# Emitting the search of blocks 2 and 3 to its end with the last four tiles of the first projection piece, ahead of the long search

## The chip, the cores and the metric

One core of a Trainium2 chip runs the whole kernel. Its engines are TensorE (PE, with PEld for its weight loads), VectorE (DVE), ScalarE (ACT), GpSimd (POOL) and SyncE (SP, which only issues DMAs here). The metric is the device time of one execution in microseconds; the time of a kernel is the median over its runs.

## What is computed

One decoder layer of 1024 tokens with 1024 channels in float32: a SwiGLU feed-forward block with LayerNorm, a token mixer with LayerNorm, a second SwiGLU block with LayerNorm. The part that matters is the mixer's sparse attention:

```
def block(i):                         # 128 queries; blocks i = 0..7
    t = i * 128 + arange(128)
    causal = key_pos[None, :] <= t[:, None]
    logit = einsum('bqhd,bsd->bqhs', qib, ki) * IDX_DIM ** -0.5
    score = einsum('bqh,bqhs->bqs', wib, relu(logit))      # 4 indexer heads
    score = where(causal[None], score, -inf)
    _, sel = lax.top_k(score, 256)
    ... softmax attention of 8 heads over the 256 selected keys
```

Blocks 0 and 1 have at most 256 causal keys, so nothing has to be chosen there. Blocks 2 to 7 need the 256 largest of 384, 512, 640, 768, 896 and 1024 scores for each query. The other half of the mixer is a gated MLP over chunks of 128 tokens; both halves are multiplied by an output matrix.

## The kernel before

All matmuls are done as three products of a high and a low part (`mm3`: lines 152, 153, 154), with the split made by ACT (high part, line 87) and DVE or POOL (low part, line 88). The program is written as Python that emits instructions in an order; a planner then decides, from the emission order as a rank, from the dependences and from its own times, in which order each engine runs them. An instruction of low rank can so run early where an engine is free and its inputs and buffers are there. SBUF buffers come from shared sets: 21 pages of 4 KB a partition hold nearly all that is named here (scores, relu results, u, v, queries, keys, masks, ranks), and an instruction whose result needs a page waits until one is free. PSUM has four single banks (projections, transposes) and two double ones (index logits, attention scores).

The mixer runs in this order. Tokens are handled in eight tiles of 128.

1. Piece A of the input projection (384 columns: latent, index weights, index key, first 188 columns of v), token tiles 0 to 3 while the first feed-forward block ends (`indexer_operands`, `piece("A")`; 24 matmuls a tile, results taken from PSUM by ACT in lines 1096 to 1100). Index queries and keys of tiles 0 to 3, then `early()`: the scores of blocks 2 and 3, and the short search over them.
2. Tail of the feed-forward block with 1 + 2 + 2 steps of the short search (`PX`), the latent normalisation (`latent`), index queries of tiles 4 to 7.
3. Tiles 4 to 7 of piece A. After each tile: `P0` steps of the short search, the index key of the tile (`keys`, transposes kT, line 719), the scores of the block with that number (`scores`: logits lg in line 703, relu on ACT in line 795, weighting on DVE in lines 798 and 800, causal mask on POOL in line 801).
4. The long search over blocks 7, 5, 4, 6 is added to the list of searches. Pieces B (418 columns: rest of v in line 1133, part of u in line 1134) and C (418 columns: rest of u, line 1141), the gate (sv, line 932) with its normalisation (vn, lines 913 to 918), the attention queries (q, lines 693 to 697), the output product of the gate half (y, xr, line 962), q_abs (qa), and the attention: four pairs of blocks by two groups of heads by two blocks, softmax (sc, line 1000), probabilities transposed (pT) and multiplied with the latent (ol). In between stand `pump(n)` calls, n taken from the lists `B`, `C`, `Q`, `W`, `A`.

A search (`topk`) is a Python generator. Its steps: the first count, 31 rounds, one for each bit of the threshold, a fix, and for each block four steps that make the mask. A round flips a bit (DVE line 845), counts the scores below the trial threshold for each block (on DVE line 826; on ACT line 835 with a sign function for block 3 of the short search and for blocks 7 and 5 of the long one), compares (DVE line 838) and keeps or drops the bit (DVE line 847). The mask's steps are a last sign count (ACT line 876), the mask itself (POOL line 881), the ties (DVE line 885, a scan `rank` in line 887, lines 889 and 891) and the sum (POOL line 892). With block 3 come the two pages that hold the masks of blocks 3 to 7. The short search has 1 + 31 + 1 + 8 = 41 steps, the long one 49.

The call that hands out the steps advances every search that is in the list by one step, so that two searches move in step:

```
def pump(self, n):
    for _ in range(n):
        for g in list(self.bg):
            try:
                next(g)
            except StopIteration:
                self.bg.remove(g)
...
for t, _ in enumerate(piece, 4):      # in indexer_operands: tiles 4 to 7
    self.pump(PAR["P0"])
    keys(t, 1)
    if PAR["SI"]:
        self.scores(t)
```

Of the kernel before, what the change touches and what calls it, by code (L numbers as in the profile page):

```python
# [13 lines left out]
ALU = mybir.AluOpType  # L14
AX = mybir.AxisListType

PAR = {'NP': 21, 'NW': 2, 'NB': 15, 'P0': 3, 'B': [0, 0, 0, 0, 0, 0, 0, 2], 'C': [0, 1, 0, 0, 0, 0, 1, 0], 'Q': [6, 0, 0, 1], 'W': [1, 4, 1, 3, 3, 4, 0, 0], 'A': [3, 0, 4, 3, 2, 3, 0, 5, 2, 0, 3, 1, 0, 1, 0, 2], 'L': 3, 'PN': [1, 1, 1, 1], 'E': 4, 'O': [0, 1, 2, 3], 'AQ': 4, 'D4': 2, 'M7': 2, 'NK': [2, 4, 6, 8], 'AK': 5, 'TP': 0, 'CUT': [384, 0, 512, 256], 'LS': 12, 'LX': 5, 'LP': 5, 'LE': [0, 0, 1, 1, 1, 0, 1], 'SE': 0, 'TE': 1, 'HE': 0, 'W2S': 0, 'W2L': 0, 'HL': 0, 'CV': 1, 'WO': 11, 'S6': 1, 'WJ': 8, 'HJ': 8, 'EO': 1, 'EN': 1, 'PX': [1, 2, 2], 'SI': 1, 'FG': 6, 'XR': [0, 2, 0, 0, 0, 1, 0, 1], 'QA': [0, 0, 0, 1, 0, 0, 0, 1, 0, 1, 0, 0, 0, 0, 0, 0], 'HT': 3, 'KO': [7, 5, 4, 6], 'K1': [1, 1], 'K1B': [4], 'K2': [2], 'K2B': [], 'S1': 1, 'LG': [1, 1, 0, 0, 1, 0, 1, 1, 1, 1, 0, 1, 1, 1], 'XV': [0, 1, 1, 0, 0, 0, 1]}
P = 128
T = 1024
D = 1024  # L20
# [9 lines left out]

N_PAGES = PAR["NP"]
N_W = PAR["NW"]
N_BIG = PAR["NB"]
EARLY = 6
class Net:
# [221 lines left out]
    def ffn(self, name, w13, w2, begin, meanwhile, load_acc, norm, after, side=iter(())):  # L257
# [21 lines left out]
        def left(n):  # L279

            for g, m in plan[len(lefts) : n]:
                if g < EARLY and m in (1, 2):
                    lefts[g, m] = self.parts(first_blocks[g, m], V)
                    continue
                a = blocks[g]
                if m == 6:
                    a[5] = self.page("S", (P, 2, HALF))
                    V.tensor_tensor(a[5], a[7], a[4], ALU.add)
                    a[6] = a[1]
                    V.tensor_tensor(a[7], a[1], a[7], ALU.subtract)  # L290
                    V.tensor_tensor(a[6], a[5], a[1], ALU.subtract)  # L291
                if m == (5 if g else 3):
                    V.tensor_tensor(a[2], a[2], a[6], ALU.subtract)
                    a[3] = a[2]
                lefts[g, m] = self.parts(a[m], E(PAR["LE"][m - 1] if g > 1 else 0))

# [18 lines left out]
        def product(g, m, ps, start=True):  # L315
            now = plan.index((g, m))
            for k in range(4):
# [6 lines left out]
                if k or now > 2 * EARLY + 4:  # L324
                    left(now + (3 if now < 2 * EARLY + 5 else 1 + (k + PAR["LS"]) // 4))
                w, x = lefts[g, m], xs[m, k]
# [44 lines left out]
        def group(g, begun=None):  # L371
# [65 lines left out]
            def out():  # L437
                e = E(PAR["HE"])
                s = c
                e.tensor_tensor(s[:, 0], h2[:, 0], h2[:, 1], ALU.add)  # L440
                e.tensor_tensor(s[:, 1], s[:, 0], h11, ALU.subtract)
                e.tensor_tensor(h2[:, 0], h11, h2[:, 0], ALU.subtract)
                e.tensor_tensor(s4, s[:, 1], h12, ALU.subtract)
                if g < EARLY:
                    nc.sync.dma_start(hid[g, :, 1], h12)
                else:
                    nc.sync.dma_start(hid[g, :, 0:2], h1)
                for i, t in enumerate((h2, s), 1):
                    nc.sync.dma_start(hid[g, :, 2 * i : 2 * i + 2], t)
                nc.sync.dma_start(hid[g, :, 6], s4)  # L450
# [795 lines left out]
```

## Time and profile before

| what | value |
|---|---|
| median of 3 runs | 1772.27 us (1771.32 to 1774.21) |
| profiled execution, its time | 1773.37 us |
| its span, first to last instruction | 1771.7 us |
| mean granted clock of TensorE | 0.995 |
| busy: PE, DVE, ACT, POOL | 1723.8, 1329.5, 791.8, 397.9 us |
| first FFN; mixer; second FFN, about | 0 to 656; 656 to 1120; 1120 to 1772 us |

Times in the profile are microseconds from the span's start. A row of an engine's list in time has the start, the duration, the engine, the line, the operation, the tiles (out<-in) and, in brackets, how long the engine stood idle before it and on whose end. A row of a view of a line or a group has a count behind the x and the durations in ns. A row of the stretches gives the busy time and, in brackets, the number of instructions of each engine.

### The profile page before, as it was taken

The page shows a single profiled execution, that of the slowest core. Times are in us where ns is not written, and L with a number is a line of the kernel's source. Part 1 is how long each engine was busy: PE and PEld are TensorE (multiplying, and loading weights), DVE is VectorE, ACT ScalarE, POOL GpSimd, SP SyncE. Part 2 cuts the span into 40 slices and gives each one's busy share as a digit, 9 for nine tenths or more (in the row PEclk, how much of TensorE's full clock was granted, in tenths as well). Part 3 has the DMA queues.
Part 4 walks back from the last instruction along what each step waited for, and adds up shares of the span by engine and source line. Part 5 has one row for each costly group of instructions (what it writes and reads, how often), then busy time and mean ns, then how long its engine had stood idle before and what let it go on. Part 6 is the DMA issues. An engine that isn't in the chain of part 4 may idle for free.

```text
span 1771.7 us, 22241 instructions
## 1 busy us (share of the span) xinstructions
PE 1723.8 (97%) x8016; PEld 1444.5 (82%) x8016; DVE 1329.5 (75%) x2220; ACT 791.8 (45%) x1347; POOL 397.9 (22%) x288
## 2 busy tenths in 40 slices
PE   8989999999999999999999999999999999999997
PEld 6868778888888888998877888888788888888886
DVE  5779886665895865899879877877777455589586
ACT  5423333423545515777777662452322222355551
POOL 0004332222000361001256321100423222200036
PEclk9999999999999999999999999999999999999999
DMA  7458767757545343224512007335443322753532
GB/s 286 152 223 295 298 257 266 268 197 285 192 126 182 102 160 123 90 87 158 199 54 96 1 1 254 120 119 202 155 166 133 123 90 89 289 194 126 176 101 83
DMA packets 89709, 288.64 MB, mean 163 GB/s; under 512 B 9088, under 2 KB 9600, under 8 KB 85504
## 3 DMA queue, kind: packets, MB, share of 16 engines
q1 hardware_dynamic: 82208, 252.33, 40.3%
q10 hardware_dynamic: 5472, 32.02, 4.5%
q0 software_dynamic: 1920, 2.89, 0.8%
q8 instruction: 63, 1.03, 0.2%
q14 instruction: 46, 0.38, 0.1%
HBM read 195.15 MB, written 89.16 MB: 160 GB/s over the span
## 4 chain that ended last, share of the span: by engine, by line
PE 69%; DVE 8%; ACT 3%; POOL 3%; issue 2%; DMA 2%; SPq 0%; POOLq 0%; ACTq 0%; DVEq 0%
PE ab L152 11%; PE ab L153 11%; PE ab L154 11%; PE y L152 5%; PE y L153 5%; PE y L154 5%; PE z L152 2%; PE z L153 2%; PE z L154 2%; PE pN L152 2%; PE pN L153 2%; PE pN L154 2%; PE tr L1013 1%; ACT act L835 1%; POOL xacc L596 1%
## 5 line engine op out<-in xcount | busy, mean ns | idle before, releaser
L152 PE MATMUL ab<-xs,hi 128*128 128x512 f32 x1232 | 482.4, 392 | 20.6 <-DVE c L416 7.7
L153 PE MATMUL ab<-xs,hi 128*128 128x512 f32 x1232 | 481.4, 391 | 0.0
L154 PE MATMUL ab<-xs,lo 128*128 128x512 f32 x1232 | 481.1, 391 | 0.0
L152 PEld LDWEIGHTS ab<-xs,hi 128*128 128x128 f32 x1232 | 232.7, 189 | 73.6 <-issue 14.4
L154 PEld LDWEIGHTS ab<-xs,lo 128*128 128x128 f32 x1232 | 232.6, 189 | 48.3
L153 PEld LDWEIGHTS ab<-xs,hi 128*128 128x128 f32 x1232 | 232.4, 189 | 48.4 <-DVE xs L88 0.4
L88 POOL TENSOR_TENSOR lo<-w,hi 128x1024 fp32r<-128x1024 f32 x54 | 139.4, 2581 | 558.7 <-ACT hi L87 532.4
L87 ACT ACTIVATE hi<-w 128x1024 fp32r<-128x1024 f32 (+1 forms) x134 | 137.6, 1040 | 161.0 <-DVE w L291 121.8
L88 DVE TENSOR_TENSOR lo<-w,hi 128x1024 fp32r<-128x1024 f32 (+1 forms) x80 | 94.8, 1195 | 42.5 <-ACT hi L87 41.6
L88 DVE TENSOR_TENSOR a<-hid,a 128x512 fp32r<-128x512 f32 x132 | 93.8, 710 | 26.9 <-ACT a L87 26.7
L87 ACT ACTIVATE a<-hid 128x512 fp32r<-128x512 f32 x132 | 81.9, 621 | 53.1 <-DMA hid<-f 49.7
L153 PE MATMUL y<-b,a 128*128 128x512 f32 x264 | 102.7, 389 | 0.0
L154 PE MATMUL y<-b,a 128*128 128x512 f32 x264 | 102.7, 389 | 0.0
L153 PE MATMUL z<-b,a 128*128 128x512 f32 x264 | 102.7, 389 | 0.0
L154 PE MATMUL z<-b,a 128*128 128x512 f32 x264 | 102.7, 389 | 0.0
L152 PE MATMUL z<-b,a 128*128 128x512 f32 x264 | 102.5, 389 | 0.0
L88 DVE TENSOR_TENSOR b<-w,b 128x512 fp32r<-128x512 f32 x110 | 77.4, 704 | 33.2 <-ACT b L87 33.0
L152 PE MATMUL y<-b,a 128*128 128x512 f32 x264 | 102.0, 389 | 0.0
L835 ACT ACTIVATE act<-score,tk 128x768 int8<-128x768 f32 (+2 forms) x93 | 87.1, 936 | 27.7 <-DVE tk L847 19.9
L349 ACT ACTIVATE h<-c 128x512 f32<-128x512 f32 x34 | 21.4, 630 | 164.6 <-DVE c L416 115.0
L87 ACT ACTIVATE b<-w 128x512 fp32r<-128x512 f32 x110 | 68.4, 622 | 52.6 <-PE z L154 38.5
L593 POOL TENSOR_TENSOR xacc<-xacc,T 128x512 f32<-128x512 f32 x8 | 13.0, 1652 | 333.8 <-DVE T L566 166.9
(267 smaller groups left out, 3573.8 us busy)
## 6 DMA issues: line engine op xcount, KB each, us to landing
w<-in_ffn_w_dram SPq DMA_DIRECT2D x110, 512.0 KB, 6.1
hid<-f SPq DMA_DIRECT2D x60, 512.0 KB, 3.8
w<-in_ffn_w_dram SPq DMA_DIRECT2D x22, 1024.0 KB, 11.5
f<-h SPq DMA_DIRECT2D x32, 512.0 KB, 3.6
made<-made ACTq DMA_DIRECT2D x16, 1024.0 KB, 6.5
f<-c SPq DMA_DIRECT2D x22, 512.0 KB, 3.8
wo<-made SPq DMA_DIRECT2D x8, 1024.0 KB, 7.5
xr<-x_spill SPq DMA_DIRECT2D x16, 512.0 KB, 4.5
```

Of the source, the lines that this page charges most:

```text
L87: nc.scalar.activation(hi, src, AF.Copy)
L88: (eng or nc.vector).tensor_tensor(lo, src, hi.bitcast(F32), ALU.subtract)
L152: mm(out, a[0], b[0], start=start, stop=False, skip_group_check=skip)
L153: mm(out, a[0], b[1], start=False, stop=False, skip_group_check=skip)
L154: mm(out, a[1], b[0], start=False, stop=stop, skip_group_check=skip)
L349: nc.scalar.activation(t, c[:, 0], AF.Silu)
L593: nc.gpsimd.tensor_tensor(acc[j][:, HALF:], acc[j][:, HALF:], T[j], ALU.add)
L596: nc.gpsimd.tensor_tensor(acc[4 + j][:, s], acc[4 + j][:, s], T[j], ALU.add)
L835: nc.scalar.activation(out, s, AF.Sign, bias=fj, scale=-1.0, accum_out=val[:, j : j + 1])
L1013: nc.tensor.transpose(pt[:, hh * P : (hh + 1) * P], ps4[hh][:, j * P : (j + 1) * P], self.ident)
```

## The change

One number in the list of parameters, the steps of the search behind each of the tiles 4 to 7 of piece A:

```diff
-PAR = {'NP': 21, 'NW': 2, 'NB': 15, 'P0': 3, ...
+PAR = {'NP': 21, 'NW': 2, 'NB': 15, 'P0': 9, ...
...
```

With 5 steps in the tail and 4 x 9 behind the tiles, all 41 steps of the short search are emitted before the long search begins; before, 5 + 4 x 3 = 17 were, and the other 24 came with the steps of the long search in the later `pump` calls, whose numbers are as they were.

More of the change, by code (lines that the diff above doesn't have):

```diff
@@ L15 @@
 AX = mybir.AxisListType
-PAR = {'NP': 21, 'NW': 2, 'NB': 15, 'P0': 3, 'B': [0, 0, 0, 0, 0, 0, 0, 2], 'C': [0, 1, 0, 0, 0, 0, 1, 0], 'Q': [6, 0, 0, 1], 'W': [1, 4, 1, 3, 3, 4, 0, 0], 'A': [3, 0, 4, 3, 2, 3, 0, 5, 2, 0, 3, 1, 0, 1, 0, 2], 'L': 3, 'PN': [1, 1, 1, 1], 'E': 4, 'O': [0, 1, 2, 3], 'AQ': 4, 'D4': 2, 'M7': 2, 'NK': [2, 4, 6, 8], 'AK': 5, 'TP': 0, 'CUT': [384, 0, 512, 256], 'LS': 12, 'LX': 5, 'LP': 5, 'LE': [0, 0, 1, 1, 1, 0, 1], 'SE': 0, 'TE': 1, 'HE': 0, 'W2S': 0, 'W2L': 0, 'HL': 0, 'CV': 1, 'WO': 11, 'S6': 1, 'WJ': 8, 'HJ': 8, 'EO': 1, 'EN': 1, 'PX': [1, 2, 2], 'SI': 1, 'FG': 6, 'XR': [0, 2, 0, 0, 0, 1, 0, 1], 'QA': [0, 0, 0, 1, 0, 0, 0, 1, 0, 1, 0, 0, 0, 0, 0, 0], 'HT': 3, 'KO': [7, 5, 4, 6], 'K1': [1, 1], 'K1B': [4], 'K2': [2], 'K2B': [], 'S1': 1, 'LG': [1, 1, 0, 0, 1, 0, 1, 1, 1, 1, 0, 1, 1, 1], 'XV': [0, 1, 1, 0, 0, 0, 1]}
+PAR = {'NP': 21, 'NW': 2, 'NB': 15, 'P0': 9, 'B': [0, 0, 0, 0, 0, 0, 0, 2], 'C': [0, 1, 0, 0, 0, 0, 1, 0], 'Q': [6, 0, 0, 1], 'W': [1, 4, 1, 3, 3, 4, 0, 0], 'A': [3, 0, 4, 3, 2, 3, 0, 5, 2, 0, 3, 1, 0, 1, 0, 2], 'L': 3, 'PN': [1, 1, 1, 1], 'E': 4, 'O': [0, 1, 2, 3], 'AQ': 4, 'D4': 2, 'M7': 2, 'NK': [2, 4, 6, 8], 'AK': 5, 'TP': 0, 'CUT': [384, 0, 512, 256], 'LS': 12, 'LX': 5, 'LP': 5, 'LE': [0, 0, 1, 1, 1, 0, 1], 'SE': 0, 'TE': 1, 'HE': 0, 'W2S': 0, 'W2L': 0, 'HL': 0, 'CV': 1, 'WO': 11, 'S6': 1, 'WJ': 8, 'HJ': 8, 'EO': 1, 'EN': 1, 'PX': [1, 2, 2], 'SI': 1, 'FG': 6, 'XR': [0, 2, 0, 0, 0, 1, 0, 1], 'QA': [0, 0, 0, 1, 0, 0, 0, 1, 0, 1, 0, 0, 0, 0, 0, 0], 'HT': 3, 'KO': [7, 5, 4, 6], 'K1': [1, 1], 'K1B': [4], 'K2': [2], 'K2B': [], 'S1': 1, 'LG': [1, 1, 0, 0, 1, 0, 1, 1, 1, 1, 0, 1, 1, 1], 'XV': [0, 1, 1, 0, 0, 0, 1]}
 P = 128
```

## The prediction

> **What bounds the kernel now.** I read the page's first part, then the busy times in stretches around the search of the top keys, then the in-order list of PE for its gaps, then the search's own lines. The page:
>
> ```profile
> span 1771.7 us, 22241 instructions
> PE 1723.8 (97%) x8016; PEld 1444.5 (82%) x8016; DVE 1329.5 (75%) x2220; ACT 791.8 (45%) x1347; POOL 397.9 (22%) x288
> ```
>
> PE is busy for 1723.8 of 1771.7 us at an almost full clock, so a change that leaves the matmuls alone can only fill or widen PE's 48 us of gaps. The stretches (first A-tile 4 to the scores' end, pieces B and C with the gate, the output product of the gate half, the head of attention, its DVE-heavy part):
>
> ```profile
> core 0: us, PE busy (x) PEld busy (x) DVE busy (x) ACT busy (x) POOL busy (x), PEclk, DMA share, GB/s
> 702.00:748.00 46.00, 43.70 (x236) 40.69 (x235) 40.48 (x145) 32.31 (x84) 3.39 (x6) 1.00 0.31 109
> 748.00:830.00 82.00, 79.52 (x424) 75.06 (x423) 76.46 (x271) 61.03 (x134) 6.27 (x6) 1.00 0.30 114
> 830.00:898.00 68.00, 67.90 (x307) 56.05 (x306) 59.24 (x153) 48.97 (x88) 18.69 (x16) 1.00 0.48 160
> 898.00:932.00 34.00, 29.57 (x153) 23.74 (x151) 22.32 (x74) 28.51 (x72) 17.64 (x28) 1.00 0.21 54
> 932.00:982.00 50.00, 45.82 (x268) 38.69 (x266) 48.98 (x121) 34.50 (x80) 29.91 (x29) 1.00 0.22 85
> ```
>
> PE loses 2.3, 2.5, 0.1, 4.4 and 4.2 us in them. From 932 to 982 DVE is the bound (48.98 of 50); in 702 to 748 and 748 to 830 it is near it (88% and 93%). The gaps that a search could have caused, from PE's list in order of time:
>
> ```profile
> 747.09 0.46 PE L152 MATMUL pN<-wN,act 128*128 128x418 f32 x1 [1.25 <-ACT u L1134]
> 800.29 0.35 PE L152 MATMUL sv<-vn,ws 128*128 128x256 f32 x1 [0.71 <-DVE u L932]
> 814.85 0.35 PE L152 MATMUL sv<-vn,ws 128*128 128x256 f32 x1 [1.18 <-DVE u L932]
> 817.00 0.38 PE L152 MATMUL sv<-vn,ws 128*128 128x256 f32 x1 [0.51 <-DVE gml L88]
> 935.80 0.50 PE L152 MATMUL sc<-cTh,act 128*128 128x512 f32 x1 [0.96 <-DVE m L1000]
> 946.32 0.50 PE L153 MATMUL ol<-pT,ch 128*128 128x512 f32 x1 [1.56 <-DVE pT L88]
> 969.20 0.44 PE L152 MATMUL sc<-cTh,act 128*128 128x384 f32 x1 [0.47 <-DVE m L1000]
> 977.00 0.41 PE L152 MATMUL sc<-cTh,act 128*128 128x320 f32 x1 [1.00 <-DVE m L1000]
> ```
>
> That is 1.25 us at the start of piece B, 2.40 us at the gate and 3.99 us in attention: 7.6 us in all, and no more can be won. The 898 to 932 gaps are q_abs and the first softmaxes, where next to no search step ran on DVE.
>
> **The change part by part.** Nothing is added or removed: 41 steps of the short search (blocks 3 and 2) stay 41. A first count is 1 step, the 31 bits are 31, a fix is 1, each block's finish is 4. Five steps are emitted in the tail of the first FFN; with 3 a tile 12 more came with A-tiles 4 to 7 (17, that is 16 rounds) and 24 later, in step with the long search. Now 36 come with those tiles, so all 41 stand ahead of the long search. No DMA is among them; the queues they pass are DVE's, ACT's and POOL's.
>
> *How far ahead the short search already ran.* The rows of its compare (two columns wide; the long search's is four wide) in 702 to 748, 748 to 830 and 830 to 898, and of its counts:
>
> ```profile
> L838 DVE TENSOR_TENSOR tk<-tk,tk x18: 130/160/176, 702.4 to 735.6; 128x2 int32<-128x2 f32 x18
> L838 DVE TENSOR_TENSOR tk<-tk,tk x30: 134/161/164, 751.4 to 829.9; 128x4 int32<-128x4 f32 x16, 128x2 int32<-128x2 f32 x14
> L838 DVE TENSOR_TENSOR tk<-tk,tk x17: 134/164/1533, 829.9 to 891.9; 128x4 int32<-128x4 f32 x17
> L826 DVE TENSOR_SCALAR_CACHE_REDUCE dve<-score,tk 128x384 int8<-128x384 f32 x18 | 10.9, 606 | 0.0
> L826 DVE DVE_READ_ACCUMULATOR dve<-score,tk 128x1 f32 x18 | 1.5, 83 | 0.0
> L845 DVE TENSOR_SCALAR tk<-tk 128x2 int32<-128x2 int32 x18 | 3.0, 166 | 0.4
> L838 DVE TENSOR_TENSOR tk<-tk,tk 128x2 int32<-128x2 f32 x18 | 2.8, 158 | 2.0 <-ACT act L835 1.5
> L847 DVE SCALAR_TENSOR_TENSOR tk<-tk,tk 128x2 int32<-128x2 int32 x17 | 2.7, 157 | 0.3
> ```
>
> By 748 the 18th round is counted though 16 were emitted: the planner fills free slots, so emission sets a rank and not a time. What moves is 13 rounds, the fix and the two finishes. One round takes DVE 0.606 + 0.083 + 0.166 + 0.158 + 0.157 = 1.17 us, 13 take 15.2. DVE had 46.00 - 40.48 = 5.5 us free in the stretch, room for 4.7 rounds. So I expect round 22 or 23 at 748, the last about 760. The finishes follow; on POOL they and what is behind them were:
>
> ```profile
> 824.53 1.58 POOL L881 TENSOR_SCALAR bias<-score,tk 128x384 bf16<-128x384 f32 x1 [49.45 <-DVE tk L847]
> 827.73 1.12 POOL L697 DMA_DIRECT2D q<-ql  x2 [1.61 <-DVE ql L695]
> ...
> 879.29 1.16 POOL L892 TENSOR_TENSOR bias<-bias,eq 128x512 bf16<-128x512 bf16 x1 [10.50 <-DVE eq L891]
> ```
>
> The first mask was begun at 824.5 and the last one done at 880; I expect about 762 and 770.
>
> *Loss: the scores of blocks 4 to 7 fall behind.* Their DVE work now ranks below every round. Who waits is seen on ACT and PE:
>
> ```profile
> 731.34 0.43 ACT L1133 ACTIVATE v<-pN 128x324 f32<-128x324 f32 x1
> 746.79 0.53 ACT L1134 ACTIVATE u<-pN 128x94 f32<-128x94 f32 x3
> 745.44 0.39 PE L703 MATMUL lg<-kil,qi 128*128 128x512 f32 x1
> ```
>
> The first B tile's v part leaves PSUM at 731.34, its u part at 746.79, three at once, just after the last score matmul (745.44). I read this as u waiting for one of the 21 pages, which ki and qi free; the PSUM banks of three B tiles wait with it, and PE stands 1.25 us. Whatever the scores' end slips, PE loses one for one. Bounds: nothing, if the extra rounds fall in the 5.5 free us; 15.2 - 5.5 = 9.7 us, if all 13 go ahead of the last score operation. Both kinds already mix in these 46 us and no DVE operation can be interrupted: I take five extra rounds, each keeping a score operation waiting for half a count (0.3 us): **+1.5 us**, nearest the lower bound, because most of those rounds have free time.
>
> *Gain or loss at the gate (the sv gaps, 800 to 817).* The short search's DVE work leaves, but the long one, alone, runs denser. From the rows, its 16 compares in 82 us are one in 5.1 us, its 17 in the 62 us after 829.9 one in 3.65. Bounds: +2.1 (one long round's two counts more ahead of the gate) and -2.4 (all three gaps gone). I take **-0.5**. The normalised halves of v here also need pages; the masks of blocks 3 to 7 take two pages some 60 us earlier, and block 3's score gives one back. That is one page more in use until about 825, which makes the second half's normalisation wait for the first half's gate; piece C's tiles 6 and 7 are the cover for PE, and without it the cost would be within the +2.1.
>
> *Gain in attention.* Long rounds at 5.1 us until 770 and 3.65 after it, started 2 us late: about 3 + 16.4 compares by 830 instead of 16, a lead of 3.4 x 3.65 = 12 us, so the search ends at about 885 and its first finishes fall before 900. Those finishes, in 932 to 982 (stretch views of lines 885, 887, 889, 891):
>
> ```profile
> 932.00:982.00 50.00, 2.55 (x4) 1.00 0.22 85
> 932.00:982.00 50.00, 7.84 (x4) 1.00 0.22 85
> 932.00:982.00 50.00, 1.28 (x4) 1.00 0.22 85
> 932.00:982.00 50.00, 4.26 (x4) 1.00 0.22 85
> ```
>
> 15.9 us of DVE for blocks 4 to 7. Blocks 4 and 5 are (640 + 768) / 3328 of the columns, 6.7 us; that share (42%) of the 3.99 us of gaps is 1.7 us. Bounds: 0 (no page is free for them before the queries are used up) and -4.0 (all leave). I take **-1.7**.
>
> *POOL and ACT.* Moved with it: two mask builds and two mask sums on POOL and the short search's counts on ACT. POOL is busy for 6.27 of 82 us where they land, and the queries' transfers on its queue come only from 827.7: nothing. ACT's counts leave 748 to 830 (61.03 of 82) for 736 to 765, where they stand between evacuations, each a few tenths late against three spare banks: nothing beside the first term.
>
> Sum: +1.5 - 0.5 - 1.7 = -0.7 us. The profiled execution took 1773.4 us, 1.1 above the median of the three runs; 1772.3 - 0.7 = **1771.6 us**.
>
> **The rivals.** *Faster:* the long search, freed of its partner, ends by 880 and finds pages, so that all four finishes leave the DVE-bound stretch: -4.0 there, half the gate's 2.4, and the scores lose nothing: 1772.3 - 5.2 = 1767.1. For it: DVE has 8.8 us free in 830 to 898 and 11.7 in 898 to 932. Against it: the queries take pages from about 900, and blocks 6 and 7 are the larger part.
>
> *Slower:* the scores give way. If the rounds keep their rank until the last score, half of the 9.7 us bound and then some goes into the 747 gap: +6 us, the long search starts 6 us later and its lead is gone: 1778. It decides from the point where the first u evacuation comes later than about 749 (the 2.2 us of gains spent). For it: DVE is 88% busy there, and a relu page is freed only by the DVE operation that waits. Against it: only 4.7 rounds fit in at all without displacing, and 18 rounds passed the same scores before at a cost of 1.25 us.
>
> *Slower by lost overlap:* two searches side by side fill each other's waits, one alone leaves DVE 8.8 of 68 us idle (830 to 898) against 5.5 of 82. If the long search so ends later, its finishes stay in the DVE-bound stretch and 82 us x (13% - 7%) = 5 us of DVE work lands there: 1777. Against it: the long round got faster alone, not slower. The Trainium skill's Perfetto Trace Analysis (Optimization Strategy) says that kernels with several regimes may gain by interleaving them, which speaks for this rival; the trace's 5.1 against 3.65 us a round speaks against it.
>
> *No effect:* the planner already ran two rounds ahead of emission; if readiness alone decides, the same order comes out: 1772.
>
> **How the numbers follow.** 0.2% (3.5 us) is about what a measurement tells here: faster is below 1768.7, slower above 1775.8. Forecast 0.38, no effect 0.05: same 0.43. Faster 0.29. Scores give way 0.22, lost overlap 0.06: slower 0.28. The likeliest alone spans 1769 to 1775; to leave no more than 2 in 10 out, the range goes into both sides' rivals, 1765.5 to 1780.
>
> **What would show it.** The two-wide compares end by 765 and the short search's mask sums by 775 (step one). First u evacuation: 747 to 749 right, beyond 751 the slower rival. The four-wide compares after 770 every 3.5 to 4 us and the last near 882: right; at 892 or later, no lead. Scans of rank before 900: two for the forecast, none if pages fail, four for the faster rival. PE's gaps in the DVE-bound stretch: 2 to 3 us instead of 4. I am wrong if PE gains a gap over 3 us before 830, or if a stretch after 1060 moves by more than 2 us, since nothing above reaches that far.

## The result and the profile after

The changed kernel is slower: 1795.39 us, the median of 4 runs (1794.25 to 1796.46), against 1773.24 us of the kernel before in 4 runs. The ratio is 1.0124, 95% interval 1.0112 to 1.0136. The profiled executions have spans of 1771.7 and 1794.7 us, 23.0 apart. The head of the page after:

```profile
span 1794.7 us, 22260 instructions
PE 1729.6 (96%) x8016; PEld 1449.2 (81%) x8016; DVE 1335.9 (74%) x2220; ACT 791.8 (44%) x1347; POOL 397.6 (22%) x288
```

No engine has more instructions to do. PE is busy for 5.8 us more with the same 8016 matmuls, and it stands still for 17.2 us more (65.1 instead of 47.9). The stretches where the prediction looked, and the piece of the second one that matters:

```profile
core 0: us, PE busy (x) PEld busy (x) DVE busy (x) ACT busy (x) POOL busy (x), PEclk, DMA share, GB/s
702.00:748.00 46.00, 43.70 (x237) 40.97 (x235) 40.03 (x161) 34.17 (x92) 3.98 (x8) 1.00 0.32 111
748.00:830.00 82.00, 65.45 (x330) 62.30 (x331) 75.61 (x224) 51.18 (x113) 9.15 (x7) 0.90 0.15 54
...
756.00:770.00 14.00, 0.33 (x1) 0.33 (x2) 13.03 (x46) 5.99 (x15) 5.23 (x4) 0.65 0.00 1
```

From 756 to 770 PE is busy for 0.33 us while DVE is busy for 13.03 of 14. Before 748 nothing is lost. PE's list in order of time has the gaps (with two rows of the time in between), and from 845 on it shows those of before again, first 22.4 us later and, from the gap that stood at 930.86 before, 23.0 us later:

```profile
708.53 0.33 PE L719 MATMUL kT<-ident,k 128*128 128x128 f32 x1 [0.69 <-ACT k L1099]
...
749.18 0.46 PE L152 MATMUL pN<-wN,act 128*128 128x418 f32 x1 [2.46 <-DVE cTl L88]
749.85 0.46 PE L152 MATMUL pN<-wN,act 128*128 128x418 f32 x1
753.23 0.42 PE L153 MATMUL pN<-wN,act 128*128 128x418 f32 x1
...
769.67 0.79 PE L703 MATMUL lg<-kih,qi 128*128 128x512 f32 x1 [14.11 <-ACT relu L795]
772.82 0.63 PE L703 MATMUL lg<-kil,qi 128*128 128x512 f32 x1
774.70 0.46 PE L152 MATMUL pN<-wN,act 128*128 128x418 f32 x1 [1.25 <-ACT u L1134]
...
1089.19 0.50 PE L152 MATMUL ol<-pT,ch 128*128 128x512 f32 x1 [0.74 <-ACT pT L87]
```

The first and the last of these matmuls stood in the trace before at:

```profile
705.81 0.33 PE L719 MATMUL kT<-ident,k 128*128 128x128 f32 x1 [0.69 <-ACT k L1099]
...
1066.23 0.50 PE L152 MATMUL ol<-pT,ch 128*128 128x512 f32 x1 [0.74 <-ACT pT L87]
```

So 2.7 us were there before anything that the edit touches, and 22.96 at 1089: 20.2 us come from between. Both executions run the same matmuls in the same order up to there, and another run of the changed kernel had a span 2 us shorter; some 1.5 of the 2.7 us come from the stretch from 33 to 37, where PE's granted clock was 0.57 in this execution and 1.00 in that of the kernel before. The three gaps are 17.82 us where 1.25 stood: +16.6. The rest is mostly a slow PE: the matmuls from 749.85 to 753.23 started 0.34 us apart instead of 0.19, the eight logit matmuls from 769.67 on 0.45 apart instead of 0.23, 1.5 us each. That makes 19.6 of the 20.2. The other 0.6 are the step from 22.4 to 23.0: PE's granted clock was 0.50 from 948 to 951, and 1.00 for the same work before (925 to 928).

Why the logits waited 14 us is read from the chain of waits, from the view that follows it back in time (start, duration, what), here the pieces around the end of the rounds:

```profile
761.35 0.17 DVE tk L838
761.54 0.17 DVE tk L847
...
766.83 0.17 DVE tk L864
767.02 0.79 DVE tk L865
767.85 0.05 issue
767.90 0.81 ACT act L876 x2
768.71 0.92 ACT relu L795
769.63 0.04 issue
769.67 3.79 PE lg L703 x8
```

and from ACT's list:

```profile
761.80 0.61 ACT L876 ACTIVATE act<-score,tk 128x384 int8<-128x384 f32 x1 [0.48 <-DVE tk L847]
767.90 0.72 ACT L876 ACTIVATE act<-score,tk 128x512 int8<-128x512 f32 x1 [5.39 <-DVE tk L865]
768.62 1.91 ACT L795 ACTIVATE relu<-lg 128x1024 f32<-128x1024 f32 x2
774.41 0.67 ACT L1134 ACTIVATE u<-pN 128x94 f32<-128x94 f32 x4
```

The relu of block 7 stands in ACT's order behind both last sign counts of the short search (line 876), so the whole short search and half of its finish are done before the last scores may go on. Nothing in the data asks for this: block 7's scores do not use blocks 2 and 3. Two of its logit tiles fill both double PSUM banks, so PE cannot make the third; behind it the first u part keeps the four single banks. What remains to be found is why the planner put that relu there.

### The profile page after: what moved, and what is told of

Same layout as the page of the kernel before. It is cut to its first block, busy times and chain, and to the rows that moved or that the text cites. A ratio compares the mean times of both kernels' runs of the same rounds, so it can differ in the third digit from the quotient of the medians.

```text
span 1794.7 us, 22260 instructions
## 1 busy us (share of the span) xinstructions
PE 1729.6 (96%) x8016; PEld 1449.2 (81%) x8016; DVE 1335.9 (74%) x2220; ACT 791.8 (44%) x1347; POOL 397.6 (22%) x288
## 4 chain that ended last, share of the span: by engine, by line
PE 74%; DVE 6%; ACT 3%; DMA 2%; issue 1%; POOL 1%; POOLq 0%; SPq 0%; ACTq 0%; DVEq 0%
PE ab L152 11%; PE ab L154 11%; PE ab L153 11%; PE y L154 5%; PE y L152 5%; PE y L153 5%; PE z L152 3%; PE z L154 3%; PE z L153 3%; PE pN L152 2%; PE pN L153 2%; PE pN L154 2%; PE tr L1013 2%; PE pT L152 1%; PE pT L154 1%
## 5 line engine op out<-in xcount | busy, mean ns | idle before, releaser
L835 ACT ACTIVATE act<-score,tk 128x768 int8<-128x768 f32 (+1 forms) x93 | 87.1, 937 | 40.8 <-DVE tk L847 36.2
```

Of the source, the lines that this page charges most:

```text
L835: nc.scalar.activation(out, s, AF.Sign, bias=fj, scale=-1.0, accum_out=val[:, j : j + 1])
```

## The experiments

Two explanations. **Shortage:** the finish of the short search takes pages (its `eq`, `rank`, and the masks) some 60 us earlier, and block 7's relu finds none of the 21 pages free. **Queue:** pages are given out in emission order, and a page's turn comes only when the instruction that first writes it is ready; with nine steps a tile, the finish's pages (ready after 31 rounds) are emitted ahead of block 7's relu and block it, free pages or not. A third, from the prediction, is that the rounds' DVE time delays the scores. The kernel before was run again beside each group: its median was 1773.8 us beside e1 to e4, 1773.6 beside e5 to e8 and 1772.8 beside e9 and e10, and the ratios below are to these.

**e1, seven steps a tile**: five and 4 x 7 are 33 steps, which is the first count, 31 rounds and the fix, and none of the finish.

```diff
-PAR = {'NP': 21, 'NW': 2, 'NB': 15, 'P0': 9, ...
+PAR = {'NP': 21, 'NW': 2, 'NB': 15, 'P0': 7, ...
```

> 7 steps behind each tile: 5 + 28 = 33, so all rounds and the fix of the short search stand ahead of the scores of block 7, the finishes (masks, ties, ranks, which need pages) do not. Pages theory (in the changed kernel the finishes' pages, claimed by rank, keep the relu of block 7 from its page): no gap over 3 us before 830, time 1770 to 1777. DVE theory (the rounds' rank on DVE holds the scores up): 16 of the 24 moved steps are still ahead, so about two thirds of the 22 us are lost, 1784 to 1790.

Measured: 1777.83 us, ratio 1.0024 (1.0015 to 1.0033), 0.8 us above the range for pages and 6 below that for DVE. The gap of 14 us is gone; the only one of over 1 us at piece B is

```profile
748.70 0.46 PE L152 MATMUL pN<-wN,act 128*128 128x418 f32 x1 [1.76 <-ACT u L1134]
```

Of the 24 moved steps 16 are still ahead of the long search, and the kernel loses some 4 us, not 22. In the profiled execution PE's granted clock is 0.72 from 748 to 754, and the sv gaps sum to 3.98 us instead of 2.40. The large loss hangs on the last eight steps, the finish.

**e3, eight steps a tile**: 37 steps, so block 2's finish is ahead of block 7's scores and block 3's is not.

```diff
-PAR = {'NP': 21, 'NW': 2, 'NB': 15, 'P0': 9, ...
+PAR = {'NP': 21, 'NW': 2, 'NB': 15, 'P0': 8, ...
```

> 8 steps behind each tile: 37, so the finish of block 2 (a page of ties, a page of ranks) is ahead of the scores of block 7, that of block 3 is not. Pages theory: the relu of block 7 still waits, but only for the first finish: the gap is 14 us less the 5.4 us that ACT waited for the second one, so 6 to 11 us, time 1783 to 1792. DVE theory: five sixths of the loss, 1789 to 1794; the two overlap here, and the gap's length tells them apart.

Measured: 1793.05 us, ratio 1.0104 (1.0088 to 1.012). The gap is back at about half its size, with the same waiter, as expected for pages; the time is 1 us above the range that went with it and alone would not tell the two apart:

```profile
765.36 0.79 PE L703 MATMUL lg<-kih,qi 128*128 128x512 f32 x1 [7.91 <-ACT relu L795]
```

The gaps of piece B sum to 11.6 us here, 6.2 less than with nine steps, and yet the time is only 2 us lower. The slow matmuls behind the gaps do not explain this, since both kernels have them (here the granted clock was 0.66 from 751 to 756 and 0.70 from 766 to 772). In the two profiled executions 2.8 us come back at the gate, whose sv gaps sum to 4.98 us instead of 2.22, and 1.9 us were there before 711; why the gate's gaps grow was not looked into.

**e2, the finish without pages**, nine steps: `eq` and mask 3 of the short search go to a small tile of their own, its `rank` to the unused half of block 3's score tile.

```diff
...
-            eq = self.page("eq", (P, 1024), BF16)[:, :n]
-            rank = self.page("rank")[:, :n]
+            if 3 in blocks:
+                eq, rank = self.short_eq[:, :n], self.short_rank[:, :n]
+            else:
+                eq = self.page("eq", (P, 1024), BF16)[:, :n]
+                rank = self.page("rank")[:, :n]
...
```

> 9 steps behind each tile as in the change, but the short search's finish takes no page: its ranks go to the unused half of the score page of block 3, its ties and the mask of block 3 to a tile of their own (2 KB). Pages theory: the 14 us gap is gone, 1768 to 1776. DVE theory: nothing changes, 1790 to 1798.

Measured: 1774.89 us, ratio 1.0004 (0.9995 to 1.0013). The stretch is that of the kernel before again, though all 41 steps stand ahead of the long search:

```profile
748.00:830.00 82.00, 79.41 (x422) 75.02 (x422) 77.23 (x241) 49.41 (x110) 11.39 (x9) 1.00 0.30 113
```

So DVE's time for the rounds is not the cause: the pages of the finish are. Shortage and queue are both left.

**e4, tile 7's steps behind its scores**, nine steps and the finish's pages as in the change: now the relu pages of block 7 are emitted first.

```diff
-            self.pump(PAR["P0"])
+            if t < 7:
+                self.pump(PAR["P0"])
             keys(t, 1)
             if PAR["SI"]:
                 self.scores(t)
+            if t == 7:
+                self.pump(PAR["P0"])
```

> 9 steps behind each tile, but behind the last tile they come after the scores of block 7 instead of before: all 41 steps still ahead of the long search, 9 of them (the fix's predecessor, fix and finishes among them) no longer ahead of block 7's scores. Pages theory: no long gap, 1769 to 1777, and any loss comes at the u evacuations or the normalised v. DVE theory: 27 of 36 steps still ahead of the scores, 1782 to 1790.

Measured: 1793.23 us, ratio 1.0114 (1.0098 to 1.0131), a miss. Block 7's relu is no longer late (its last one ends at 750.1), but the gap only moved to the next name in the emission order, the u page:

```profile
749.05 1.03 ACT L798 ACTIVATE relu<-lg 128x1024 f32<-128x1024 f32 x1
...
770.33 0.72 ACT L879 ACTIVATE act<-score,tk 128x512 int8<-128x512 f32 x1 [5.39 <-DVE tk L868]
771.05 0.64 ACT L1137 ACTIVATE u<-pN 128x94 f32<-128x94 f32 x4
...
771.34 0.72 PE L152 MATMUL pN<-wN,act 128*128 128x418 f32 x1 [14.13 <-ACT u L1137]
```

The last logit matmul starts at 748.13 and DVE has read the last relu by 752.0, so by then ki, qi and all relus are done with, and u still waits for the same sign count. That speaks for the queue; my recorded expectation had no long gap at all.

**e5, the pages claimed early**: e4 with five one-column writes by GpSimd behind block 7's scores, so that the finish's pages have their turn at once and are then held.

```diff
...
+                self.claimed = {0: self.page("bias", (P, 2048), BF16)}
+                for i in (2, 3):
+                    self.claimed[i] = self.page("eq", (P, 1024), BF16), self.page("rank")
+                for x in (self.claimed[0], *self.claimed[2], *self.claimed[3]):
+                    self.nc.gpsimd.memset(x[:, :1], 0.0)
...
```

> Nine steps a tile, tile 7's steps behind its scores as in the run e4_after_scores, whose gap was 14.1 us ahead of the first u page. Added: five GpSimd writes of one column right behind tile 7's scores that take the mask page and the eq and rank pages of blocks 2 and 3 early. The finish uses just as many pages as before and holds them longer; only their turn changes. Queue theory (pages go out in emission order, and a page's turn comes when its first writer is ready): the turns of the five pages are over by about 750, u's page follows at once, no PE gap over 3 us before 830, 1771 to 1778. Shortage theory (five pages fewer until the finish ends, so u has none): the gap stays at 10 to 16 us or grows, 1788 to 1800.

Measured: 1785.79 us, ratio 1.0067 (1.0055 to 1.0079): between the two forecasts. Both gaps of piece B:

```profile
749.26 0.46 PE L152 MATMUL pN<-wN,act 128*128 128x418 f32 x1 [1.75 <-ACT u L1145]
...
780.21 0.72 PE L152 MATMUL pN<-wN,act 128*128 128x418 f32 x1 [7.88 <-ACT u L1145]
```

The gap of 14 us is gone, as the queue says: u leaves PSUM at 748.94, in the middle of the rounds. But the held pages now seem to run out. The second half of the normalised v (vn, ACT line 87) starts only at 777.42, just after DVE has read block 2's rank for the last time (776.72 to 777.33); in e10 both halves are done by 765.4. The third u page (token tiles 4 and 5) follows at 779.92, just after the last reading of the first v page (to 779.79). I take this for a real shortage, of the experiment's own making; it is read from these times and no run tests it. The run does not decide by itself.

**e9 and e10, one page and its turn**: e2, in which pages are no issue, plus a single page that nothing reads, one column of it written at the first finish step. In e9 the writer needs the final threshold, in e10 it needs nothing.

```diff
...
                 eq, rank = self.short_eq[:, :n], self.short_rank[:, :n]
+                if i == 2:
+                    V.tensor_scalar(self.page("turn")[:, :1], t, -1.0, None, ALU.mult)   # e9
+                    nc.gpsimd.memset(self.page("turn")[:, :1], 0.0)                      # e10 instead
...
```

> e2_no_pages (nine steps a tile, the short finish takes no page, 1774.9, no long gap) plus a single page that nothing reads: one column of it is written once, from the final threshold, at the first step of the finish, and the page is free again at once. Queue theory (a page's turn comes in emission order and only when its first writer is ready): the relu of block 7, emitted behind it, waits for the end of the 31 rounds although pages are free: a PE gap of 11 to 15 us near 765 to 772, 1789 to 1797. Shortage theory (the finish's pages left too few): one page held for a fraction of a microsecond costs nothing, 1773.5 to 1777. Rival (the searches' DVE work delays the scores): as e2, 1773.5 to 1777.

> The control: the same page at the same place in the emission order, but its one column is set to zero by GpSimd, which waits for nothing. Queue theory: its turn passes when it comes, as e2: no gap over 3 us before 830, 1773.5 to 1777. A theory in which the page itself costs (its place among the 21, the extra instruction): as e9, whatever that is.

Measured: e9 1791.15 us, ratio 1.0105 (1.009 to 1.012); e10 1775.69 us, ratio 1.0012 (1.0003 to 1.0021). The page is written for 0.15 us and never held, and e9 is 18 us above the kernel before and 15.5 above e10. The rows of e9 (DVE's and ACT's lists, then PE's):

```profile
759.47 0.15 DVE L890 TENSOR_SCALAR turn<-tk 128x1 f32<-128x1 f32 x1
...
759.96 1.92 ACT L795 ACTIVATE relu<-lg 128x1024 f32<-128x1024 f32 x2
...
761.01 0.79 PE L703 MATMUL lg<-kih,qi 128*128 128x512 f32 x1 [8.01 <-ACT relu L795]
```

and of e10, where the same page has its turn early:

```profile
L890 POOL MEMSET turn<- x1: 88/88/88, 732.6 to 732.6; 128x1 f32 x1
...
741.50 1.02 ACT L795 ACTIVATE relu<-lg 128x1024 f32<-128x1024 f32 x1
```

The relu that follows the page in the emission order starts 0.5 us after the late write in e9 (behind block 2's sign count, as in the change), and in e10 it starts 18 us earlier. The queue is shown; a shortage cannot do this with a page that is free again at once. The time is in the range that I gave for the queue, but the gap was off: I expected 11 to 15 us, and it is 8.01 with a 1.25 behind it and 2.47 ahead of it. These three are 10.5 us more than the 1.25 before; some 4 us more are the slow matmuls behind them, told at the end.

**e6, three steps a tile without pages**, the control for e2.

> Three steps a tile as in the kernel before, with the short finish's eq, rank and mask 3 outside the pages as in e2_no_pages (1774.9). The control for e2: what nine steps do when pages are out of the way. Queue theory: e2 holds no other cost of the early search, so the two are within 2.5 us: 1772 to 1775. Rival (the early search also costs DVE time, as my prediction's term of +1.5 had it, hidden in e2 by the freed pages): 1770 to 1772, that is 3 us or more below e2.

Measured: 1773.48 us, ratio 1.0002 (0.9993 to 1.001), 0.1 below its kernel before where e2 is 1.1 above its own. With the pages out of the way, nine steps instead of three cost about 1 us and bring nothing; e10 is 2.9 above its kernel before, so at most some 3 us.

**e7 and e8, every finish off the pages**, with nine and three steps. They ask why the lead of the long search brought attention nothing: do its scans wait for pages?

```diff
...
-            eq = self.page("eq", (P, 1024), BF16)[:, :n]
-            rank = self.page("rank")[:, :n]
+            eq = self.eq[:, :n]
+            rank = self.rank[:, 512 : 512 + n] if 3 in blocks else self.rank[:, :n]
+            if i == 7:
+                eq, rank = self.rank, self.rank7
...
```

> Nine steps a tile; eq and rank of every finish, and mask 3, outside the pages (blocks 2 to 6 in a tile of their own and in the idle score tile of block 3, block 7 in the two score tiles that are done), so that only masks 4 to 7 still take two pages. Queue theory: no long gap, and the long search's lead now reaches its finish, because its scans no longer queue behind the pages of the queries and softmaxes: the scans of rank start within 15 us of the last round (before 920) and not at 934 to 974; attention's gaps fall from 4 to 1 to 3 us; 1770 to 1773.5. Rival (pages were not what held the finish, DVE was, or the two mask pages still queue): scans at 930 to 975 as before, 1773.5 to 1776.

> As e7_all_off_9 but three steps a tile, as in the kernel before. Queue theory: the last round is at about 892 as before, scans follow within 15 us, before the DVE-bound stretch begins at 932; a gain of 0.5 to 3 us over before, 1771 to 1773.5, and e7 is at or below it by up to 2 us (its lead of some 9 us). Rival: within 1 us of before, scans at 934 and later.

Measured: e7 1780.21 us, ratio 1.0038 (1.0026 to 1.005); e8 1774.48 us, ratio 1.0003 (0.9994 to 1.0012); both are above the range that I gave for the queue. One of the four long scans, that of block 4, left attention: it starts at 906.8 in e7 and 896.9 in e8 (933.7 before). So pages held the first. The other three stayed at 944 or later, and these two runs cannot tell why, because the edit gives blocks 4, 5 and 6 one `eq` tile in common. The rows of e8 (DVE's list, then POOL's):

```profile
895.20 0.55 DVE L889 TENSOR_SCALAR eq<-score,tk 128x640 bf16<-128x640 f32 x1
...
942.50 0.61 DVE L889 TENSOR_SCALAR eq<-score,tk 128x768 bf16<-128x768 f32 x1
...
938.83 1.41 POOL L896 TENSOR_TENSOR bias<-bias,eq 128x640 bf16<-128x640 bf16 x1
```

Block 5's ties are written into that tile only after POOL has added block 4's from it (to 940.24), and block 4's mask, which still takes a page, is built on POOL from 932.37 on. Whether the shared tile, the mask pages or the place in the emission order, among the `pump` calls of attention, keeps the three there stays open. Attention's gaps are no smaller. In e7 a new wait came:

```profile
911.46 0.93 ACT L878 ACTIVATE act<-score,tk 128x768 int8<-128x768 f32 x1 [4.03 <-DVE tk L865]
...
916.82 0.58 PE L152 MATMUL sc<-cTh,act 128*128 128x256 f32 x1 [5.14 <-ACT act L87]
```

ACT waited for the fix of the long search (line 865) with the queries' evacuations behind it, and PE went without; its granted clock was then 0.72 from 917 to 925. An earlier finish was put where q_abs needs ACT.

## Why the prediction was wrong

*The loss term, +1.5 us.* This is the step that failed: it measured +19.6, the gaps and the slow matmuls behind them, about twice its upper bound of 9.7. That bound was DVE time (15.2 of rounds minus 5.5 free), but the scores of block 7 did not wait for DVE time; they waited for the last round's result, because pages have an order. A wait of that kind is bounded by the end of the search, and I had that end: last round at about 760, the masks to 770. Had I put block 7's relu behind it, a long gap would have followed. I read the 21 pages as a pool and counted them, for u, for the gate and for attention, and never asked in which order they go out. The statement that a change which leaves the matmuls alone can only fill or widen PE's gaps failed as well: 3.0 of the 19.6 us are the same matmuls at half pace.

*The timing of the short search* was right. 23 two-wide compares fall in 702 to 748 where there were 18; the first is that of the first count, so 22 rounds are compared and the 23rd is counted by 748 (22 or 23 expected); the last compare is at 761.35 (about 760) and the finish's masks on POOL run from 761.9 to 772.7 (762 to 770).

*First u evacuation.* 747 to 749 would have been right, beyond 751 the slower rival: it came at 774.41. The slower rival had the right place and sign, but its mechanism (rounds that keep their rank) and its price of 6 us were wrong: e2 has the same rounds and u at 747.41. What the prediction set for and against it weighed DVE, which was not the cause.

*The gate, -0.5.* The three sv gaps sum to 2.22 us (0.44, 0.79, 0.99) instead of 2.40: inside the bounds and nearer nothing. In e2 and e10 they do not close either (1.35 and 1.34 us the largest).

*The lead and attention, -1.7.* The long rounds do run in 4.0 us alone (3.65 expected), and the 32nd compare is at 905.1, which is 9 us early against the shift of 22.4 us (12 expected). It bought nothing: the scans are later by exactly what PE is,

```profile
956.78 1.48 DVE L887 TENSOR_TENSOR_SCAN rank<-eq 128x640 f32<-128x640 bf16 x1
```

against 933.75 in the trace before, 23.0 us, and the gaps there are those of before. The lower bound held; the reason given with it (pages) is shown by e8 for the first of the four scans and open for the other three. Lost overlap did not show: a long round took 4.0 us alone and 5.1 beside the short search.

*Nothing after 1060 moves:* right; from 1066 on before and 1089 after, the two traces keep the same distance to within 0.2 us.

## What to carry to other kernels

If buffers are handed out in emission order, a step that is emitted earlier but can run only much later blocks every buffer request behind it, even for a buffer it holds for a moment. So for each moved step that asks for a shared buffer, find when its first writer can run and who asks next; the loss is bounded by that time and the slow matmuls behind the gap, not by engine time. A buffer of its own for the late step removes the block (e2), but an earlier result is worth something only if what consumes it can also move.

## What the runs showed of the hardware

A PE gap cost more than its length, and by amounts that were not in my sum. Stretches of e9, whose gap runs from about 753 to 761:

```profile
748.00:753.00 5.00, 4.83 (x24) 4.43 (x24) 4.07 (x22) 3.00 (x7) 0.00 (x0) 1.00 0.17 56
753.00:761.00 8.00, 0.01 (x1) 0.00 (x0) 6.97 (x36) 5.50 (x15) 2.57 (x2) 0.73 0.00 1
761.00:766.00 5.00, 3.78 (x8) 2.48 (x8) 5.00 (x12) 3.07 (x5) 0.01 (x1) 0.50 0.00 0
766.00:770.00 4.00, 3.95 (x11) 3.79 (x12) 4.00 (x7) 0.42 (x3) 1.91 (x1) 0.50 0.01 2
770.00:775.00 5.00, 5.00 (x27) 4.91 (x27) 5.00 (x10) 4.03 (x10) 3.12 (x2) 0.96 0.00 0
```

The granted clock (the number behind POOL's) stays at 0.50 for 9 us after an idle time of 8 us: the 19 matmuls in them took about twice their time at full speed. In the changed kernel an idle time of only 2.46 us was followed by 3.4 us of matmuls at half pace (749.85 to 753.23), while in e9 the same gap of 2.47 us at 748.17 was followed by none (1.00 from 748 to 753). So it was with 1.76 us: in e1 the granted clock was 0.50 from 750 to 753 after such a gap at 748.70, and in e10 it stayed at 1.00 from 748 to 756 around one at 751.11. The Trainium skill's page TensorE: Matmul & The Clock Gate (section Part 1: The HAM clock gate) says that the clock is halved after an idle window of some 3.4 us, needs as long a busy one to come back, and that the windows run free of the kernel. The 3.4 us of slow matmuls agree with that, and so does it that the same gap slowed PE in one run and not in another. That the idle time must last 3.4 us does not agree: 2.46 and 1.76 us were enough. The 9 us of e9 are longer than one such window, and in the first 5 of them PE was still waiting for part of the time (3.78 busy of 5).
